# RWKV-7 and S5 decoder step on one core: S5 products and projection weight splits on VectorE, squares summed by TensorE, one function table for Ln and Exp

## The chip, the cores and the metric

The kernel runs on one of the eight cores of a Trainium2 chip. A core has a matrix engine (TensorE, PE in the rows), a vector engine (VectorE, DVE), an engine for activation functions (ScalarE, ACT), a general engine (GpSimd, POOL) and a queue that issues the transfers (SyncE, SP). Each runs its own list of instructions in order, and semaphores make one wait for another. The metric is the device time of one execution in microseconds (us), as the median of the runs.

## The reference, cut to what matters

One layer for a prompt of 1024 tokens and eight single-token samples, in float32. The two groups are joined to 1032 columns.

```python
h = rmsnorm(x, ln1_g); proj = h @ w_in       # 1024 -> 1792 (RWKV) + 512 (S5 input u) + 2048 (gates)
# RWKV-7: token shift, decay, normalised keys kk / |kk|, a matrix state per head, group norm of y
# S5: bu = B u per group, then s[t] = A s[t-1] + bu[t] in complex numbers, y = Re(C s) + D u
z = gelu(y_s5); zz = z @ w_glu; s5_out = zz[:, :D] * sigmoid(zz[:, D:])
x = x + (sigmoid(g_rw) * (y_rw @ w_rw_out) + sigmoid(g_s5) * s5_out) @ w_out
x = x + conv_ffn(rmsnorm(x, ln2_g))          # 1024 -> 2 x 2816, causal conv of width 3, gelu gate, down
x = x + sigmoid(rmsnorm(x, ln3_g) @ w_ple_gate) * (p @ w_ple)
y = rmsnorm(x, final_g)                      # rmsnorm: x * rsqrt(mean(x * x) + eps) * g
```

## The kernel before

Channels lie on the 128 partitions, tokens on the columns. A large product is exact to float32 in three faster passes: each operand is split into a rounded part "hi" and the rest "lo", and PE adds hi*hi, hi*lo and lo*hi in PSUM (mmblk). For the weights, ScalarE makes whi as a rounded copy and GpSimd makes wlo = raw - whi, 128x512 at a time (wload, line 490). A tile of the input projection takes 128 output channels: eight pieces of depth, three blocks of 344 columns, so 24 matmuls of 344 columns to a block. Its result in PSUM ("psm") is multiplied by rstd and carried to SBUF by VectorE: as "ut" for the four S5 input tiles, "pt" for the 14 RWKV tiles, "gt" for the 16 gate tiles. Eight low-rank products (xp, wp) are carried out by ScalarE ("st").

At the start, the eight pieces of x (128x1032, "xin") are scaled and split into h1h and h1l; ScalarE squares x in place (line 593); GpSimd adds the squares of pieces 1 to 3 and VectorE those of 5 to 7 into two sums, VectorE adds the two, and three fp32 products with a matrix of 1/1024 put the mean on all partitions ("pst", rstd1_ from line 600). rsqrt is Ln and then Exp, times -0.5 (line 527). Until rstd is there no projection block leaves PSUM: tile 0 has one block each in the pools pch, py and pb, and tile 1 has the three of pm.

The S5 part (build_s5) makes tables of powers of A (pr, pi, Q), the products wt, wx (for B) and cd, wy (for C), then the inputs of the state (be), and then runs the recurrence by cmac, which multiplies complex numbers in four products and four sums: first over 4 places at a time (three steps of 128x512), then over longer distances on VectorE alone, then back (four groups of 128x372). In the long steps two of the four products, ts[2] and ts[3], are on GpSimd. The first product of the outputs is "yp".

After that comes the RWKV stage, eight units of one head pair and half the tokens, each with several reciprocal roots and exponentials; the gate tiles and then the GLU fill PE between its small products. Behind it, two halves of 512 and 520 tokens run through the output products and the ConvFFN.

The order on each engine is not written by hand. Every operation is recorded by Sched.rec (all operations have line 413) with a priority, and Sched.run picks for the engine that is free first the ready operation with the lowest priority number, by estimated costs; S5 and RWKV (SIDE) go ahead of the projection tiles (MAIN), and results carried out of PSUM (HI) ahead of both. In Sched.issue a function that isn't in the present table set makes ScalarE switch: SETS lists the sets that hold a function, and the first of the list is taken.

```python
SETS = {"Exp": (0, 6), "Tanh": (0, 11), "Ln": (5, 6), "Gelu_apprx_tanh": (11,), "Sin": (9,)}
if o.aset and self.aset not in o.aset:
    self.aset = o.aset[0]
```

Of the kernel before, what the change touches and what calls it, by code (L numbers as in the profile page):

```python
# [17 lines left out]
P = 128  # L18
# [83 lines left out]
class Sched:  # L102
# [273 lines left out]
    def issue(self, t, o):  # L376
        e = o.eng
        self.pend[e].remove(o)
        cost = o.cost
        if o.aset and self.aset not in o.aset:  # L380
            self.aset = o.aset[0]
            t += 1283
        if o.mode and o.mode != self.mode:
            self.mode = o.mode
            t += self.SWITCH
        if o.port:
            t = max(t, self.held["POOL" if e == "DVE" else "DVE"] - 190)
            self.held[e] = t + o.lat
        for nm in o.alloc:
            q, _ = self.tile_slot[nm]  # L390
            q[0].remove(min(q[0]))
            q[1].remove(nm)
        self.free[e] = t + cost
        if e == "SP":
            st = max(self.dma_free, t + 900)
            self.dma_free = st + o.tail
            end = self.dma_free + 1300
        else:
            end = t + o.lat
        o.ready, o.nd = end, -1  # L400
        for u in o.users:
            u.ready = max(u.ready, end + self.lat(o, u))
            u.nd -= 1
            if u.nd == 0:
                self.pend[u.eng].append(u)
        for nm in o.tiles:
            self.left[nm] -= 1
            if self.left[nm] == 0:
                q, _ = self.tile_slot[nm]
                q[0].append(end + 250)  # L410
        for p in o.pools:
            self.pool_left[p] -= 1
        o.fn(*o.args, **o.kw)  # L413
        o.users = o.args = o.kw = None
# [11 lines left out]
def build(tc, I, O, dbg=None):  # L426
# [50 lines left out]
    def wload(src, n=W4):  # L477
        wp, nr, nw, alt = wts["pool"]
        wts["n"] = wts.get("n", 0) + 1
        with g.prio(HI):  # L480
            if alt and wts["n"] % 2:
                raw = wp.tile([P, TW], F32, name="wraw", tag="ta", bufs=2)
                G.memset(raw[:, 0:1], 0.0)
            else:
                raw = wp.tile([P, W4], F32, name="wraw", tag="wraw", bufs=nr)
            dma(raw[:, :n], src)
            hi = wp.tile([P, W4], F32R, name="whi", tag="whi", bufs=nw)
            S.activation(hi[:, :n], raw[:, :n], AF.Copy)
            lo = wp.tile([P, W4], F32R, name="wlo", tag="wlo", bufs=nw)
            G.tensor_tensor(lo[:, :n], raw[:, :n], hi[:, :n].bitcast(F32), op=SUB)  # L490
        return [(hi[:, j * P:(j + 1) * P], lo[:, j * P:(j + 1) * P]) for j in range(n // P)]

    def wtiles(src, nk):
# [39 lines left out]
    hs = ExitStack()  # L533
    hp = pool(hs, "hp", side="right")
    wts["pool"] = hp, 2, 3, True

    def slot(name, dt=F32R, shape=(NT,), tag="h"):
        t = hp.tile([P] + list(shape), dt, name=name, tag=tag, bufs=16 if tag == "h" else 1)
# [34 lines left out]

    XT = ("ur", "cdl", "yf", "xs", "zt", "cd", "wx", "ut")
    with g.prio(HI):
        acc, wpre = [], [wtiles(I["w_in"][M_U[0]], 8)]
        for k in range(8):
            if k == 4:
                wpre.append(wtiles(I["w_in"][M_U[1]], 8))
            x = sp.tile([P, NT], F32, name="xin", tag=XT[k], bufs=1)  # L580
            if XT[k] in ("xs", "zt", "cd"):
                V.memset(x[:, 0:1], 0.0)
            elif XT[k] in ("wx", "ut", "yf", "cdl"):
                G.memset(x[:, 0:1], 0.0)
            dma(x, I["x"][k])
            hi, lo = slot("h1h"), slot("h1l")
            if k % 2 == 0:
                V.tensor_scalar(hi, x, pc("ln1", k), None, op0=MUL)
            else:
                S.activation(hi, x, AF.Copy, scale=pc("ln1", k))  # L590
            V.scalar_tensor_tensor(lo, x, pc("ln1", k), hi.bitcast(F32), op0=MUL, op1=SUB)
            with g.prio(HI + 1):
                S.activation(x, x, AF.Square)
                if k in (0, 4):
                    acc.append(x)
                else:
                    (G if k < 4 else V).tensor_tensor(acc[-1], acc[-1], x, op=ADD)
            hx.append((hi, lo))

    def rstd1_():  # L600
        with g.prio(HI):
            for b in range(3):
                ps = pb.tile([P, BL], F32, name="pst", tag="big")
                sl = slice(b * BL, (b + 1) * BL)
                V.tensor_tensor(acc[0][:, sl], acc[0][:, sl], acc[1][:, sl], op=ADD)
                T.matmul(ps, ones, acc[0][:, sl], start=True, stop=True)
                rsqrt(rstd1[:, b * BL:(b + 1) * BL], ps, epst[:, 0:1])


    def win(m, evac, pools=None):  # L610
# [26 lines left out]
    def u_tile(q):  # L637
# [5 lines left out]
        def ev(b, sl, ps):  # L643
# [5 lines left out]
            if b == 2:  # L649
                V.tensor_tensor(ut[:, 0, 136:144], ps[:, 336:344], rstd1[:, NP:], op=MUL)  # L650
                V.tensor_tensor(ut[:, 7, 0:8], ps[:, 336:344], rstd1[:, NP:], op=MUL)
        win(M_U[q], ev, ((pch, "ch"), (py, "Y"), (pb, "big")) if q == 0 else None)
        with g.prio(HI):
            dma(dap(Ud[q], 0, [[144, P], [16 * 1152, 8], [1, 144]]), ut)

# [56 lines left out]
    for p in (2, 3):  # L712
        proj_tile(M_K[p])
        proj_tile(M_R[p])
        proj_tile(M_V[p])
    for m in M_GS + M_GR:
        gate_tile(m)

# [253 lines left out]
def build_s5(g, sp, pb, cp, I, O, Ud, Zd, pcs, dscr, dap, dma):  # L972
# [112 lines left out]
    frb = t["fr"][:, :, None].to_broadcast([P, 32, 16])  # L1085
    fib = t["fi"][:, :, None].to_broadcast([P, 32, 16])
    tt(v1, frb, Br, MUL)
    G.tensor_tensor(v2, fib, Bi, op=MUL)
    tt(b1, v1, v2, SUB)
    tt(v1, frb, Bi, MUL)  # L1090
    tt(v2, fib, Br, MUL)
# [13 lines left out]
    for q in range(4):  # L1105
# [3 lines left out]
        wx = tl("wx", [8, 9, 16], tag="wx")  # L1109
        V.tensor_tensor(wt, prr[:, gs, :, None].to_broadcast(sh),  # L1110
                        b1[:, gs, None, :].to_broadcast(sh), op=MUL)
        G.tensor_tensor(wx[:, :, 0:8], pir[:, gs, :, None].to_broadcast(sh),
                        b2[:, gs, None, :].to_broadcast(sh), op=MUL)
        V.tensor_tensor(wt, wt, wx[:, :, 0:8], op=ADD)
        bt = tl("bt", [8, 128], tag="bt")
# [9 lines left out]
        for i0 in (0, 3, 6):  # L1125
# [5 lines left out]
            for h in range(2):  # L1131
# [3 lines left out]
                for dst, r in zip(Xe, (0, 64)):  # L1135
# [3 lines left out]
                    else:  # L1139
# [4 lines left out]
        V.tensor_tensor(cd, q1[:, gs, :, None].to_broadcast(sh),  # L1144
                        Cr[:, gs, None, :].to_broadcast(sh), op=MUL)
        wx = tl("wy", [8, 9, 16], tag="ys")
        G.tensor_tensor(wx, q2[:, gs, :, None].to_broadcast(sh),
                        Ci[:, gs, None, :].to_broadcast(sh), op=MUL)
        V.tensor_tensor(cd, cd, wx, op=ADD)
        cdd = dscr(f"cdd{q}", [P, 8, 9, 16])  # L1150
# [20 lines left out]
        "p (a b c) -> p a b c", b=n[1], c=n[2]) if len(n) == 3 else \  # L1171
        m[i][:, :math.prod(n)].rearrange("p (a b) -> p a b", b=n[1])

    def cmac(outr, outi, ar, ai, br, bi, ts, small=False):
        E = V if small else G
        E.tensor_tensor(ts[2], ar, bi, op=MUL)
        V.tensor_tensor(ts[0], ar, br, op=MUL)
        E.tensor_tensor(ts[3], ai, br, op=MUL)
        V.tensor_tensor(ts[1], ai, bi, op=MUL)
        V.tensor_tensor(outr, outr, ts[0], op=ADD)  # L1180
        V.tensor_tensor(outi, outi, ts[2], op=ADD)
# [7 lines left out]
    for v in range(1, 4):  # L1189
        cmac(xv[0][:, :, :, v, 3], xv[1][:, :, :, v, 3], *qb(3, 8),  # L1190
             xv[0][:, :, :, v - 1, 3], xv[1][:, :, :, v - 1, 3],
             [mv(j, 16, 8) for j in range(4)], True)
    for u in range(1, 8):
        cmac(xv[0][:, :, u, 3, 3], xv[1][:, :, u, 3, 3], Qr[:, :, 15], Qi[:, :, 15],
             xv[0][:, :, u - 1, 3, 3], xv[1][:, :, u - 1, 3, 3],
             [m[j][:, :16] for j in range(4)], True)
    for v in range(3):
        cmac(xv[0][:, :, 1:, v, 3], xv[1][:, :, 1:, v, 3], *qb(4 * v + 3, 7),
             xv[0][:, :, :7, 3, 3], xv[1][:, :, :7, 3, 3],
             [mv(j, 16, 7) for j in range(4)], True)  # L1200

    x0 = tl("x0", [2, 16, 8])
    dma(x0, I["s5x0"])
# [1 line left out]
    dma(x0s, I["s5x0s"])  # L1205
    mv8 = [mv(j, 16, 8) for j in range(4)]
    ab8 = lambda z: z[:, :, None].to_broadcast([P, 16, 8])
    cmac(er, ei, ab8(apr), ab8(api), x0[:, 0], x0[:, 1], mv8, True)

    for i, e in enumerate((er, ei)):  # L1210
        S.activation(x0[:, i], e, AF.Copy)
# [520 lines left out]
```

## Time and profile before

| what | value |
| --- | --- |
| runs | 1912.15, 1913.16 and 1919.73 us, median 1913.16 |
| profiled execution | 1906.36 us |
| its span, from the first to the last instruction | 1904.6 us |
| mean granted TensorE clock | 0.973 of full speed |
| PE, DVE, ACT, POOL busy | 1829.4, 1159.5, 832.3, 847.0 us |
| function-table loads on ACT | 68, 87.2 us in all |

Busy is the time in which an engine has an instruction under way. Matmuls overlap each other, so a busy PE need not be at its full pace, and the count of matmuls in a stretch says more. An fp32 product shows as two matmul records.

### The profile page before, as it was taken

The numbers are of one execution on the slowest core, as the hardware profiler recorded it, in microseconds if no ns is written. First come the engines' busy times: TensorE is split into PE (matmuls) and PEld (weight loads), VectorE is DVE, ScalarE is ACT, GpSimd is POOL, SyncE is SP. The second block draws the span as 40 slices with busy tenths as digits, with TensorE's granted clock in tenths as the row PEclk, the third lists the DMA queues.
The fourth block names the chain that finished last, engine by engine and source line by source line (L and its number), as shares of the span: only waits on it lengthen the run. The fifth ranks groups of instructions, "written<-read, shape, count | busy, mean of one in ns | idle before, by whom it ended". The sixth has DMA issues, their size and how long they took to land.

```text
span 1904.6 us, 32427 instructions
## 1 busy us (share of the span) xinstructions
PE 1829.4 (96%) x11904; PEld 1624.1 (85%) x11904; DVE 1159.5 (61%) x2333; ACT 832.3 (44%) x1461; POOL 847.0 (44%) x1151
## 2 busy tenths in 40 slices
PE   6998899999999999999999999999999999999987
PEld 5987899877878889887788888888899999999987
DVE  8998527678666578777655534447555445444565
ACT  5232435346355465645633333335545333323354
POOL 4453325223223243336655454546564444444454
PEclk9998999899799999999999999999999999999988
DMA  5453684322123255344633333323332233233322
GB/s 189 145 169 113 186 256 130 112 78 81 53 78 95 74 176 158 90 156 137 211 101 113 114 97 97 94 94 112 100 123 78 90 92 98 90 95 96 90 70 87
DMA packets 157950, 219.81 MB, mean 115 GB/s; under 512 B 48208, under 2 KB 81488, under 8 KB 157648
## 3 DMA queue, kind: packets, MB, share of 16 engines
q1 hardware_dynamic: 157792, 217.74, 36.7%
q8 instruction: 94, 1.54, 0.3%
q14 instruction: 64, 0.52, 0.1%
HBM read 174.94 MB, written 42.92 MB: 114 GB/s over the span
## 4 chain that ended last, share of the span: by engine, by line
PE 77%; DVE 9%; DMA 6%; ACT 3%; issue 2%; POOL 1%; SPq 1%; DVEq 0%; POOLq 0%; ACTq 0%
PE psm L413 65%; PE chp L413 4%; PE Yps L413 2%; DVE Tm L413 1%; PE gp L413 1%; DVE Tt L413 1%; PE yp L413 1%; DVE x L413 1%; SPq L413 1%; DMA yf<-yq 1%; POOL wlo L413 1%; PE mgp L413 1%; ACT L413 1%; DVE m L413 1%; DVE Xi L413 1%
## 5 line engine op out<-in xcount | busy, mean ns | idle before, releaser
L413 POOL TENSOR_TENSOR wlo<-wraw,whi 128x512 fp32r<-128x512 f32 (+2 forms) x468 | 599.4, 1284 | 557.3 <-ACT whi L413 531.2
L413 PE MATMUL psm<-act,whi 128*128 128x260 f32 (+1 forms) x2880 | 655.2, 322 | 3.3 <-ACT whi L413 2.3
L413 PEld LDWEIGHTS psm<-act,whi 128*128 128x128 f32 x2880 | 480.2, 190 | 47.8 <-ACT whi L413 2.9
L413 ACT ACTIVATE whi<-wraw 128x512 fp32r<-128x512 f32 (+2 forms) x468 | 279.0, 598 | 526.5 <-PE psm L413 314.5
L413 PE MATMUL psm<-act,wlo 128*128 128x260 f32 (+1 forms) x1440 | 463.1, 322 | 0.5 <-POOL wlo L413 0.5
L413 PE MATMUL psm<-mid,whi 128*128 128x260 f32 (+1 forms) x1344 | 307.0, 321 | 2.0 <-ACT mid L413 2.0
L413 PEld LDWEIGHTS psm<-act,wlo 128*128 128x128 f32 x1440 | 273.4, 190 | 22.0 <-POOL wlo L413 0.9
L413 PE MATMUL psm<-h1h,whi 128*128 128x344 f32 x816 | 272.1, 336 | 12.9 <-DVE s_sh L413 9.7
L413 PE MATMUL psm<-h1h,wlo 128*128 128x344 f32 x816 | 274.0, 336 | 0.8 <-POOL wlo L413 0.8
L413 PE MATMUL psm<-h1l,whi 128*128 128x344 f32 x816 | 272.1, 334 | 2.0 <-DVE h1l L413 2.0
L413 PEld LDWEIGHTS psm<-mid,whi 128*128 128x128 f32 x1344 | 223.4, 189 | 23.5 <-ACT mid L413 2.6
L413 PE MATMUL psm<-mid,wlo 128*128 128x260 f32 (+1 forms) x672 | 214.6, 322 | 0.5 <-POOL wlo L413 0.5
L413 PEld LDWEIGHTS psm<-h1h,whi 128*128 128x128 f32 x816 | 159.0, 195 | 18.1 <-ACT s_sh L413 9.6
L413 PEld LDWEIGHTS psm<-h1l,whi 128*128 128x128 f32 x816 | 159.2, 195 | 4.9 <-DVE h1l L413 2.5
L413 PEld LDWEIGHTS psm<-h1h,wlo 128*128 128x128 f32 x816 | 159.1, 195 | 4.6 <-POOL wlo L413 1.1
L413 DVE TENSOR_TENSOR x<-psm,x 128x260 f32<-128x260 f32 (+1 forms) x160 | 84.6, 532 | 121.6 <-PE psm L413 121.5
L413 PEld LDWEIGHTS psm<-mid,wlo 128*128 128x128 f32 x672 | 126.5, 188 | 10.8 <-POOL wlo L413 0.9
L413 DVE TENSOR_TENSOR ta<-psm,rs 128x260 f32<-128x260 f32 (+1 forms) x66 | 34.0, 517 | 143.0 <-PE psm L413 131.1
L413 DVE SCALAR_TENSOR_TENSOR cv<-ta,par,cv 128x512 f32<-128x512 f32 x88 | 88.8, 1009 | 40.5 <-ACT cv L413 39.0
L413 ACT ACT_TABLE_LOAD x68 | 87.2, 1283 | 1.9 <-PEq L1723 0.7
L413 DVE TENSOR_TENSOR mid<-cv,mid 128x260 fp32r<-128x260 f32 (+1 forms) x84 | 69.5, 832 | 29.1 <-ACT mid L413 28.8
L413 ACT ACTIVATE sw<-S,WC 64x64 f32<-64x64 f32 x120 | 41.3, 344 | 73.1 <-DVE S L413 71.4
(346 smaller groups left out, 2578.0 us busy)
## 6 DMA issues: line engine op xcount, KB each, us to landing
wraw<-in_w_ffn_in SPq DMA_DIRECT2D x176, 256.0 KB, 2.6
wraw<-in_w_in SPq DMA_DIRECT2D x68, 256.0 KB, 3.5
wraw<-in_w_ffn_out SPq DMA_DIRECT2D x64, 192.0 KB, 2.4
gd<-gt SPq DMA_DIRECT2D x16, 516.0 KB, 3.1
wraw<-in_w_out SPq DMA_DIRECT2D x32, 256.0 KB, 2.7
wraw<-in_w_ple_gate SPq DMA_DIRECT2D x32, 256.0 KB, 2.7
wraw<-in_w_ffn_out SPq DMA_DIRECT2D x32, 256.0 KB, 3.0
pd<-pt SPq DMA_DIRECT2D x12, 516.0 KB, 3.4
```

Source lines behind the costliest of these rows:

```text
L413: o.fn(*o.args, **o.kw)
```

## The change

Four things change. In wload the low part of the weights is made by the engine in wts["lo"]: VectorE for the 18 tiles of S5 input and RWKV, GpSimd from the gate tiles on. In build_s5 all products are on VectorE: v2, wx, wy, and ts[2] and ts[3] of every cmac. The squares of x are summed by 24 fp32 products into three PSUM blocks that are taken from pb before the loop; tile 0 of the projection has a block of pm in place of the one of pb. And where a function is in set 6, which holds Ln and Exp, that set is loaded.

```diff
@@ issue
         if o.aset and self.aset not in o.aset:
-            self.aset = o.aset[0]
+            self.aset = 6 if 6 in o.aset else o.aset[0]
+            if self.aset == 6 and len(o.aset) > 1:
+                self.nc.scalar.preload_act_table_set("natural_log_exp_and_others")
             t += 1283
@@ wload
-            G.tensor_tensor(lo[:, :n], raw[:, :n], hi[:, :n].bitcast(F32), op=SUB)
+            wts["lo"].tensor_tensor(lo[:, :n], raw[:, :n], hi[:, :n].bitcast(F32), op=SUB)
@@ build
     wts["pool"] = hp, 2, 3, True
+    wts["lo"] = V
...
-        acc, wpre = [], [wtiles(I["w_in"][M_U[0]], 8)]
+        wpre = [wtiles(I["w_in"][M_U[0]], 8)]
+        pst = [pb.tile([P, BL], F32, name="pst", tag="big") for _ in range(3)]
         for k in range(8):
...
                 S.activation(x, x, AF.Square)
-                if k in (0, 4):
-                    acc.append(x)
-                else:
-                    (G if k < 4 else V).tensor_tensor(acc[-1], acc[-1], x, op=ADD)
+            for b in range(3):
+                T.matmul(pst[b], ones, x[:, b * BL:(b + 1) * BL], start=k == 0, stop=k == 7)
...
             for b in range(3):
-                ps = pb.tile([P, BL], F32, name="pst", tag="big")
-                sl = slice(b * BL, (b + 1) * BL)
-                V.tensor_tensor(acc[0][:, sl], acc[0][:, sl], acc[1][:, sl], op=ADD)
-                T.matmul(ps, ones, acc[0][:, sl], start=True, stop=True)
-                rsqrt(rstd1[:, b * BL:(b + 1) * BL], ps, epst[:, 0:1])
+                rsqrt(rstd1[:, b * BL:(b + 1) * BL], pst[b], epst[:, 0:1])
...
-        win(M_U[q], ev, ((pch, "ch"), (py, "Y"), (pb, "big")) if q == 0 else None)
+        win(M_U[q], ev, ((pch, "ch"), (py, "Y"), (pm, "psm")) if q == 0 else None)
...
+    wts["lo"] = G
     for m in M_GS + M_GR:
         gate_tile(m)
@@ build_s5
-    G.tensor_tensor(v2, fib, Bi, op=MUL)
+    tt(v2, fib, Bi, MUL)
...
-        G.tensor_tensor(wx[:, :, 0:8], pir[:, gs, :, None].to_broadcast(sh),
+        V.tensor_tensor(wx[:, :, 0:8], pir[:, gs, :, None].to_broadcast(sh),
...
-        G.tensor_tensor(wx, q2[:, gs, :, None].to_broadcast(sh),
+        V.tensor_tensor(wx, q2[:, gs, :, None].to_broadcast(sh),
...
-    def cmac(outr, outi, ar, ai, br, bi, ts, small=False):
-        E = V if small else G
-        E.tensor_tensor(ts[2], ar, bi, op=MUL)
+    def cmac(outr, outi, ar, ai, br, bi, ts):
+        V.tensor_tensor(ts[2], ar, bi, op=MUL)
         V.tensor_tensor(ts[0], ar, br, op=MUL)
-        E.tensor_tensor(ts[3], ai, br, op=MUL)
+        V.tensor_tensor(ts[3], ai, br, op=MUL)
```

Since the order follows from costs and readiness, it changes along with the work. On ScalarE, where rstd of the first norm is made (xin are the squares, rstd Ln and Exp of the sums), this stands there before:

```order
L413 ACTIVATE whi<-wraw 128x512 x2
L413 ACT_TABLE_LOAD
L413 ACTIVATE rstd_71<-pst,epst 128x344 x2
L413 ACT_TABLE_LOAD
L413 ACTIVATE rstd_71<-rstd_71 128x344 x2
L413 ACT_TABLE_LOAD
L413 ACTIVATE rstd_71<-pst,epst 128x344
L413 ACT_TABLE_LOAD
L413 ACTIVATE rstd_71<-rstd_71 128x344
```

and this in the change:

```order
L415 ACTIVATE xin<-xin 128x1032 x4
L383 ACT_TABLE_LOAD
L415 ACTIVATE rstd_71<-pst,epst 128x344 x2
L415 ACTIVATE rstd_71<-rstd_71 128x344 x2
L415 ACTIVATE rstd_71<-pst,epst 128x344
L415 ACTIVATE rstd_71<-rstd_71 128x344
```

Four loads became one, and the split of the weights (whi) moved from ahead of rstd to behind it.

On PE the sums of squares (pst) stand between the projection products of the first tiles (psm), before behind 144 of these:

```order
L413 MATMUL psm<-h1l,whi 128x344
L413 MATMUL psm<-h1h,wlo 128x344
L413 MATMUL pst<-xin,ones 128x344 x3
L413 MATMUL psm<-h1h,whi 128x344
L413 MATMUL psm<-h1l,whi 128x344
L413 MATMUL psm<-h1h,wlo 128x344
```

and in the change behind 35 of them:

```order
L415 MATMUL psm<-h1h,wlo 128x344
L415 MATMUL psm<-h1l,whi 128x344
L415 MATMUL pst<-xin,ones 128x344 x24
L415 MATMUL psm<-h1h,whi 128x344
L415 MATMUL psm<-h1l,whi 128x344
L415 MATMUL psm<-h1h,wlo 128x344
```

All 24 stand in one piece, and the products that wait for no rstd, 85 of them, are behind it.

On VectorE, in the first steps of the S5 recurrence (m are the products, Xr and Xi the states, pt a projection block carried out of PSUM), this stands there before, from one pt to the second next:

```order
L413 TENSOR_TENSOR pt<-psm,rstd_71 128x344
L413 TENSOR_TENSOR m_656<-Qr,Xr 128x512
L413 TENSOR_TENSOR m_657<-Qi,Xi 128x512
L413 TENSOR_TENSOR Xr<-Xr,m_656 128x16x32
L413 TENSOR_TENSOR pt<-psm,rstd_71 128x344
L413 TENSOR_TENSOR Xi<-Xi,m_658 128x16x32
L413 TENSOR_TENSOR Xr<-Xr,m_657 128x16x32
L413 TENSOR_TENSOR Xi<-Xi,m_659 128x16x32
L413 TENSOR_TENSOR m_656<-Qr,Xr 128x512
L413 TENSOR_TENSOR pt<-psm,rstd_71 128x344
```

and in the change from one pt on, the next one standing two rows behind the last shown:

```order
L415 TENSOR_TENSOR pt<-psm,rstd_71 128x344
L415 TENSOR_TENSOR m_659<-Qi,Xr 128x512
L415 TENSOR_TENSOR wlo<-wraw,whi 128x512
L415 TENSOR_TENSOR m_657<-Qi,Xi 128x512
L415 TENSOR_SCALAR st<-st 128x1032
L415 TENSOR_TENSOR Xr<-Xr,m_656 128x16x32
L415 TENSOR_TENSOR Xi<-Xi,m_658 128x16x32
L415 TENSOR_TENSOR Xr<-Xr,m_657 128x16x32
L415 MEMSET pt 128x1
L415 TENSOR_TENSOR Xi<-Xi,m_659 128x16x32
L415 TENSOR_TENSOR m_658<-Qr,Xi 128x512
L415 TENSOR_TENSOR m_656<-Qr,Xr 128x512
```

Two products more in each step, two of the weight splits (one shown, wlo) and a scaling (st) stand between the same evacuations.

On the other queues, SP issues the weight loads of the third tile ahead of the S5 constants (before: behind two of them), and up to the RWKV stage GpSimd has no instruction left but short fills of tiles.

## Rows read from the trace of the kernel before

**Rows 1.** Busy us of each engine, share of the span and instructions (the page)
```profile
PE 1829.4 (96%) x11904; PEld 1624.1 (85%) x11904; DVE 1159.5 (61%) x2333; ACT 832.3 (44%) x1461; POOL 847.0 (44%) x1151
```

**Rows 2.** By stage: stretch, length, busy PE, PEld, DVE, ACT, POOL, clock, DMA share
```profile
0.00:207.00 207.00, 180.48 (x1034) 164.81 (x1034) 185.02 (x383) 72.16 (x116) 96.27 (x105) 0.93 0.47 152
140.00:180.00 40.00, 33.12 (x139) 27.18 (x138) 34.59 (x90) 9.06 (x16) 16.46 (x13) 0.79 0.33 111
310.00:950.00 640.00, 627.11 (x4275) 524.25 (x4275) 446.97 (x1104) 330.21 (x581) 240.45 (x398) 0.97 0.38 115
950.00:1904.00 954.00, 928.75 (x6004) 845.11 (x6003) 486.38 (x771) 381.61 (x693) 478.50 (x582) 0.99 0.31 97
```

**Rows 3.** An undisturbed stretch, the projection products alone
```profile
60.00:80.00 20.00, 20.00 (x129) 1.00 0.47 142
```

**Rows 4.** Waits of PE up to 310 us: total us, times, longest
```profile
PE psm L413 <- DVE s_sh L413: 9.7, 1, 9.7
PE psm L413 <- DVE pt L413: 6.9, 2, 4.5
```

**Rows 5.** Timeline of VectorE: start us, us, engine, line, operation
```profile
11.54 2.49 DVE L413 SCALAR_TENSOR_TENSOR h1l<-xin,par,h1h 128x1032 fp32r<-128x1032 f32 x2
...
14.81 5.50 DVE L413 SCALAR_TENSOR_TENSOR h1l<-xin,par,h1h 128x1032 fp32r<-128x1032 f32 x2
...
113.73 1.35 DVE L413 TENSOR_TENSOR cd<-q,bc 128x1152 f32<-128x1152 f32 x1
...
142.85 0.49 DVE L413 TENSOR_TENSOR pt<-psm,rstd 128x344 f32<-128x344 f32 x1
...
148.05 1.07 DVE L413 TENSOR_TENSOR Xi<-Xi,m 128x512 f32<-128x512 f32 x1
...
149.99 0.52 DVE L413 TENSOR_TENSOR pt<-psm,rstd 128x344 f32<-128x344 f32 x1
```

**Rows 6.** Timeline of GpSimd beside the second pair of h1l
```profile
16.26 2.95 POOL L413 TENSOR_TENSOR xin<-xin 128x1032 f32<-128x1032 f32 x1 [0.41 <-ACT xin L413]
```

**Rows 7.** PE in four stretches: busy (records), granted clock, DMA share, GB/s
```profile
36.60:46.50 9.90, 3.82 (x9) 0.69 0.16 53
46.50:50.00 3.50, 3.42 (x12) 0.50 0.00 0
360.00:375.00 15.00, 13.61 (x72) 0.66 0.30 82
474.00:498.00 24.00, 24.00 (x109) 0.51 0.15 39
```

**Rows 8.** Chain of waits, S5 stage: start us, us, what, records
```profile
100.75 2.05 PE be L413 x16
```

**Rows 9.** Groups of VectorE up to 207 us: count, busy us, mean ns
```profile
L413 DVE SCALAR_TENSOR_TENSOR h1l<-xin,par,h1h 128x1032 fp32r<-128x1032 f32 x8 | 18.2, 2308 | 0.3
...
L413 DVE TENSOR_TENSOR cd<-cd,wy 128x1152 f32<-128x1152 f32 x4 | 9.1, 2287 | 0.2
...
L413 DVE TENSOR_TENSOR cd<-q,bc 128x1152 f32<-128x1152 f32 x4 | 8.2, 2060 | 0.0
...
L413 DVE TENSOR_TENSOR wt<-wt,wx 128x1024 f32<-128x1024 f32 x4 | 4.8, 1211 | 0.0
...
L413 DVE TENSOR_TENSOR wp<-wraw,wp 128x512 fp32r<-128x512 f32 x2 | 1.3, 674 | 0.0
```

**Rows 10.** Function-table loads (the page): count, busy us, mean ns, idle before
```profile
L413 ACT ACT_TABLE_LOAD x68 | 87.2, 1283 | 1.9 <-PEq L1723 0.7
```

**Rows 11.** Timeline of ScalarE in the RWKV stage
```profile
357.37 1.28 ACT L413 ACT_TABLE_LOAD   x1
358.67 0.63 ACT L413 ACTIVATE sq<-sq 128x512 f32<-128x512 f32 x1
359.20 0.57 ACT L413 ACTIVATE Gm<-mgp 32x512 f32<-32x512 f32 x1
```

**Rows 12.** Waits of PE in the RWKV stage
```profile
PE chp L413 <- ACT Gm L413: 1.5, 2, 1.0
```

More of the change, by code (lines that the diff above doesn't have):

```diff
@@ L1191, in build_s5 @@
              xv[0][:, :, :, v - 1, 3], xv[1][:, :, :, v - 1, 3],
-             [mv(j, 16, 8) for j in range(4)], True)
+             [mv(j, 16, 8) for j in range(4)])
     for u in range(1, 8):
@@ L1195, in build_s5 @@
              xv[0][:, :, u - 1, 3, 3], xv[1][:, :, u - 1, 3, 3],
-             [m[j][:, :16] for j in range(4)], True)
+             [m[j][:, :16] for j in range(4)])
     for v in range(3):
@@ L1199, in build_s5 @@
              xv[0][:, :, :7, 3, 3], xv[1][:, :, :7, 3, 3],
-             [mv(j, 16, 7) for j in range(4)], True)
+             [mv(j, 16, 7) for j in range(4)])
     x0 = tl("x0", [2, 16, 8])
@@ L1207, in build_s5 @@
     ab8 = lambda z: z[:, :, None].to_broadcast([P, 16, 8])
-    cmac(er, ei, ab8(apr), ab8(api), x0[:, 0], x0[:, 1], mv8, True)
+    cmac(er, ei, ab8(apr), ab8(api), x0[:, 0], x0[:, 1], mv8)
     for i, e in enumerate((er, ei)):
```

## The prediction

> **What bounds the kernel now.** I read the busy shares first [rows 1]: TensorE (PE) is busy 1829.4 of 1904.6 us, VectorE (DVE) 61%, GpSimd (POOL) and ScalarE (ACT) 44% each. So the end is set by PE's own work plus the time in which PE waits or runs slowly, and work of another engine counts only where PE waits for it. Next I read busy time by stage [rows 2]: from 950 us on PE has 929 of 954 us, from 310 to 950 it has 627 of 640; but from 140 to 180 us it has 33.1 of 40 at a mean granted clock of 0.79. In the first 207 us (up to the first product of the S5 outputs, "yp") DVE is busy 185 us. The pace of an undisturbed stretch is 129 matmuls in 20 us, 0.155 us each [rows 3].
>
> The waits of PE say who holds it up [rows 4]: 9.7 us before the first matmul, 6.9 us for "pt", a projection block that DVE carries out of PSUM. So PE waits because DVE comes late. Why DVE is late is seen in its timeline [rows 5]: two h1l of 1032 columns took 2.49 us (1.25 each), the next two 5.50, while GpSimd among other things added up squares [rows 6]. Between the evacuations at 142.85 and 149.99 us DVE worked 7.1 us on adds and products of the S5 recurrence; one alone takes 1.07. Instructions of DVE and POOL that both read two SBUF tiles stretch each other.
>
> A wait costs PE more than its length [rows 7]: after the idle stretch 36.6 to 46.5 us the granted clock is 0.50 (1.2 instead of 2.4 GHz) from 46.5 to 50, and 12 matmuls run where the pace gives 22.
>
> **The change part by part.** The sum goes against the profiled execution, 1906.36 us (span 1904.6 and 1.8 around it); the median of the runs, 1913.16, is 1.0036 times that.
>
> (a) Squares summed by PE. In place of 3 fp32 products there are 24 of 344 columns. Eight fp32 products of the S5 part, 136 columns each, take 2.05 us in 16 records [rows 8], 0.256 each, so 344 columns take 0.65 at full clock: 24 x 0.65 = 15.6 us, less about 3.4 now (3.82 busy, less three ordinary ones at 0.155) [rows 7]: +12. They cover no idle time: in the new order they stand in one block behind 35 projection products, where PE has other work ready. Bounds: +5 if most of it replaces waits for h1l, +28 at half clock.
>
> (b) The first product waits longer. DVE now does two weight splits before it (0.67 each, the duration of "wp", same shape [rows 9]) and the short S5 instructions that stood behind it, between 9.7 us [rows 4] and 11.5 us [rows 5]: +3. The bounds are 0 and +3.3. From there all h1l run without GpSimd beside them, so the last Square should end near 26 us (the first product at 12.7, then by DVE's rows 8 x 1.25 for h1l, three h1h at about 0.75 and one split).
>
> (c) The wait for rstd goes. From 36.6 to 46.5 us PE is busy 3.8 of 9.9, and the half clock behind it costs 1.6 (10 matmuls): -7.7. What is late next is the evacuation of the first blocks, at about 35 us (squares products from 18 to 33, then Ln, Exp); but PE then has 85 projection products (13 us) left for the five blocks that have PSUM, so it should not stop. Bounds -7.7 and -3.
>
> (d) The S5 stage, 140 to 180 us. 139 records at 0.155 are 21.5 us of the 40; I count 16 as lost, since the low-rank products among them are slower by themselves. DVE takes over 21 splits before the first yp (x 0.67 = 14), v2 and eight wx and wy (0.67 + 4 x 1.21 [rows 9] + 4 x 1.35 [rows 5] = 11), six 128x512 products (x 1.07 = 6) and eight of 372 columns (half of that each, an estimate: 4): +35. It loses the six sums of squares (3 x 1.25 + 3 x 0.42, from h1l by columns: 5) and the stretching. By group means [rows 9] that is 8 x (2.31 - 1.25) = 8.5 for h1l and 4 x (2.29 - 1.35) + 4 x (2.06 - 1.35) = 6.6 for the two cd groups: 15 from three groups; all of GpSimd's 96 busy us [rows 2] are the other end. I take 30, near the lower end, as the other groups are smaller: DVE's load stays as it is. What matters then is the spacing of evacuations. Where four instructions stand between two of them now (7.1 us), twelve stand then, by rows some 11 us (nine at 1.07, a split, a scaling at about 0.7). PE has three buffers of 24 products, 11 us of work, so it still waits, but less long: I take half of the 16, -8. Bounds -16 and +6.
>
> (e) The other waits for evacuations between 46 and 207 us, some 7 us in all: -3. Bounds -7 and +4.
>
> (f) One table for Ln and Exp. The program's order has 69 function-table loads before and 42 after, 27 x 1.28 us = 35 us less on ACT [rows 10]; not more, since each Tanh or Gelu between brings the other table back. ACT is no bound. What counts is a place like that at 357 us [rows 11]: a load and a reciprocal root stand ahead of "Gm", for which PE waits [rows 12], and from 360 to 375 us the clock is 0.66, that is 5 us lost; 474 to 498 us at 0.51, 12 us lost [rows 7], has no load just ahead of it. In the new order no load stands between the first two units: -6. Bounds +6 (another such stretch appears) and -20 (both go). The Trainium skill, page "ScalarE: Activation LUTs", section "What ACT_TABLE_LOAD costs", puts a switch at 2.66 us with its drain; here the load is 1.28 and the next instruction starts 0.02 us behind it [rows 11], so the trace does not show that drain. By the page this term would be about -9.
>
> Sum: +12 + 3 - 7.7 - 8 - 3 - 6 = -9.7. I forecast -11, as the lower bounds of (d) to (f) lie farther off than the upper ones: 1895.4, times 1.0036 is 1902 us.
>
> **Rivals.** 1, a larger gain: DVE is freed by far more than 30 us, so the waits of (d) go whole, and with them both half-clock stretches of (f): 12 + 3 - 7.7 - 16 - 5 - 17 = -31, 1882 us. For it: PE's waits named here are for DVE, and DVE is stretched by more than twice in rows 5. Against: the new spacing of evacuations.
>
> 2, a trade: what GpSimd gives up DVE has to do, one instruction after the other as before; the waits of (d) and (e) stay, and (f) gives 3: 12 + 3 - 7.7 - 3 = +4, 1917 us, no change. For it: 185 of 207 us of DVE are busy already. The Trainium skill, page "Perfetto Trace Analysis", section "Optimizing Scalar/DVE Operations", warns that moving work between these two engines might not help, since they share a read port; the rows agree on the sharing, but 1.25 against 2.75 us for one h1l says that ending the overlap gives something back.
>
> 3, slower: DVE becomes the bound of the S5 stage. It decides from the point where DVE's time to the first yp exceeds PE's. PE's is 12.7 + 742 x 0.155 + 160 short S5 records x 0.128 [rows 8] + 15.6 = 164 us; if only the 15 us of stretching counted above go, DVE's is 185 + 35 - 5 - 15 = 200 and some 8 before it has anything to do. The first yp, which with 126 products fewer ahead of it (19.5 us) would come at 187.5 at today's speed, then comes at 208: +20 with (f) at 0, 1933 us. For it: ten instructions of 1 us between two evacuations. Against: GpSimd's 96 us would then have cost DVE only 15, which rows 5 make unlikely.
>
> **How the numbers follow.** Forecast 0.5 (its own range -19 to -3 us), rival 1 0.13, rival 2 0.25, rival 3 0.12. Less than 0.5% (9.5 us) can't be told from no change: 0.37 of the forecast's half lies beyond it, which with rival 1 makes 0.50 faster; 0.13 and rival 2 make 0.38 the same; 0.12 slower. The range, 1881 to 1920, holds the forecast, rival 2 and half of rival 1.
>
> **What would show it.** (a) 24 squares products in one block, 15 to 17 us long, at clock 1.0. (b) The first matmul near 12.7 us. (c) The first "ut" near 35 us, and PE without a long gap from 13 to 50. (d) h1l at 1.25 us throughout, PE's wait for pt below 4 us, and the first yp near 183 us (187.5 less (a) to (e)). (f) 27 table loads fewer, and no clock of 0.66 near 360 us. The forecast is wrong if PE still waits 7 us or more for pt (then rival 2 or 3), or if the squares run at 1.2 GHz.

## The result, and the profile after

The changed kernel took 1924.35 us (median of 20 runs, 1911.49 to 1938.47) against 1911.9 us for the kernel before (20 runs, 1896.76 to 1921.64): ratio 1.0086, with a 95% interval of 1.0064 to 1.0108. It is slower by about 16 us (the means of the runs are 1925.5 and 1909.7); 1902 us had been forecast, with a range up to 1920. The profiled execution took 1918.17 us (span 1916.4), 11.8 more than that of the kernel before.

The page of the changed kernel, busy time by engine, to be set beside [rows 1]:

```profile
PE 1852.4 (97%) x11946; PEld 1637.8 (85%) x11946; DVE 1135.4 (59%) x2386; ACT 799.5 (42%) x1434; POOL 734.4 (38%) x1089
```

POOL lost 113 us of work and ACT 33 us, DVE gained none, and PE is busy 23 us longer. So PE's idle time fell from 75.2 to 64.0 us (span less busy), and the loss is in time in which PE is busy. Before any stage is blamed, the signs of the prediction are looked up one by one. First the waits of PE up to 310 us, to be read against [rows 4]:

```profile
PE psm L415 <- DVE h1h L415: 11.3, 1, 11.3
PE ssp L415 <- ACT kkn L415: 6.6, 1, 6.6
...
PE psm L415 <- DVE pt L415: 2.4, 3, 1.5
```

The wait for pt is down from 6.9 to 2.4 us, as forecast (below 4). The first product stands at 11.3 us (12.7 forecast, 9.7 before). Next come the squares on PE, the first block carried out by VectorE, and two h1l together (timeline of the changed kernel; three answers, of PE, DVE and DVE):

```profile
19.87 14.04 PE L415 MATMUL pst<-xin,ones 128*128 128x344 f32 x48
```
```profile
35.90 0.77 DVE L415 TENSOR_TENSOR ut<-psm,rstd 128x344 f32<-128x344 f32 x1
```
```profile
14.55 2.50 DVE L415 SCALAR_TENSOR_TENSOR h1l<-xin,par,h1h 128x1032 fp32r<-128x1032 f32 x2
```

The 24 products stand in one block. The next product starts at 33.49 us, so they take 13.6 us. The first ut comes at 35.9 us (35 forecast), and h1l takes 1.25 us everywhere, where [rows 5] had 2.75 beside GpSimd. Now the stages of the changed kernel (columns as in [rows 2]):

```profile
0.00:186.70 186.70, 169.30 (x950) 150.83 (x950) 168.67 (x421) 65.88 (x108) 4.82 (x55) 0.96 0.47 156
140.00:180.00 40.00, 39.09 (x188) 34.19 (x189) 39.07 (x153) 12.57 (x24) 0.53 (x6) 0.87 0.43 142
279.80:848.50 568.70, 557.60 (x3914) 466.56 (x3913) 389.91 (x1050) 260.66 (x482) 177.47 (x309) 0.95 0.31 94
848.50:1916.40 1067.90, 1043.50 (x6571) 941.32 (x6569) 536.81 (x844) 429.44 (x778) 538.40 (x671) 0.99 0.34 108
```

The first yp stands at 186.7 us (207.5 before, 183 forecast), and from 140 to 180 us PE has 39.09 of 40 us instead of 33.12. So most signs of the front came as the prediction says, and the loss comes later. The RWKV stage runs here from 279.8 us (first chp) to 848.5 us (last of its records). In the kernel before, the same stage and what follows are these two rows:

```profile
308.20:925.30 617.10, 606.76 (x4201) 508.63 (x4200) 435.31 (x1090) 314.49 (x554) 225.49 (x374) 0.97 0.36 108
925.30:1904.60 979.30, 950.90 (x6092) 862.22 (x6090) 499.85 (x789) 399.02 (x723) 493.45 (x605) 0.99 0.33 102
```

The stage is shorter now by 48 us, and that misleads: it also holds 305 projection products fewer (1764 instead of 2069), which come later instead. To compare stages, I take from the length of each the time that its projection products need at their undisturbed pace (0.1555 us for 344 columns, 0.118 for 260, 0.230 for 512). What remains is the price of everything else:

| remainder in us | before | changed | difference |
| --- | --- | --- | --- |
| start to first yp | 72.5 | 71.4 | -1.1 |
| to first chp | 38.5 | 38.3 | -0.2 |
| RWKV stage | 275.5 | 294.4 | +18.9 |
| rest | 56.2 | 50.4 | -5.8 |
| sum | 442.7 | 454.5 | +11.8 |

The difference of the sums is that of the two executions. In the RWKV stage the records of the granted clock show 34.1 us at half clock before and 61.4 us now; over the whole span they show 103.0 and 113.9, since the other stages have less of it now. The longest of these stretches in the changed kernel, all engines and then the projections alone (busy PE, PEld, DVE, ACT, clock, DMA):

```profile
549.80:580.50 30.70, 30.70 (x118) 22.48 (x118) 11.82 (x37) 8.62 (x19) 3.63 (x9) 0.50 0.14 38
```
```profile
549.80:580.50 30.70, 12.76 (x33) 9.23 (x33) 0.52 (x1) 0.00 (x0) 0.50 0.14 38
```

PE is busy all the time, but with 33 projections among 118 records. What came just before, in the timeline of the same kernel:

```profile
546.29 1.17 PE L415 MATMUL mgp<-av,Gm 32*32 32x32 f32 x32 [0.82 <-DVE av L415]
547.38 0.48 PE L415 MATMUL gp<-AR,BK 64*128 64x128 f32 x2
...
548.62 1.19 PE L415 MATMUL mgp<-Gm,av 32*32 32x32 f32 x32
549.74 0.78 PE L415 MATMUL gp<-AR,BK 64*128 64x128 f32 x2
550.45 2.07 PE L415 MATMUL gps<-sg,g 128*128 128x512 f32 x2
```

Small products of RWKV follow each other (32x32 in groups of 32) with four projections among them, where the dots stand, and the clock falls behind them. The function-table loads did go as forecast, from 69 (68 of them in the group of [rows 10]) to 42 (groups of ScalarE in the changed kernel):

```profile
L415 ACT ACT_TABLE_LOAD x22 | 28.2, 1283 | 1.2 <-PEq L1721 0.7
L383 ACT ACT_TABLE_LOAD x19 | 24.4, 1283 | 0.3
L332 ACT ACT_TABLE_LOAD x1 | 1.3, 1283 | 0.0
```

### The profile page after: what moved, and what is told of

The parts are those of the page before. It is cut to its first block, busy times and chain, and to the rows that moved or that the text cites. A ratio compares the mean times of both kernels' runs of the same rounds, so it can differ in the third digit from the quotient of the medians.

```text
span 1916.4 us, 32539 instructions
## 1 busy us (share of the span) xinstructions
PE 1852.4 (97%) x11946; PEld 1637.8 (85%) x11946; DVE 1135.4 (59%) x2386; ACT 799.5 (42%) x1434; POOL 734.4 (38%) x1089
## 4 chain that ended last, share of the span: by engine, by line
PE 73%; DVE 10%; DMA 4%; ACT 3%; issue 2%; POOL 1%; SPq 1%; DVEq 0%; ACTq 0%; POOLq 0%
PE psm L415 61%; PE chp L415 5%; PE Yps L415 2%; PE gp L415 1%; DVE m L415 1%; DVE act L415 1%; SPq L415 1%; DMA wraw<-in_w_rw_out 1%; PE yp L415 1%; DVE x L415 1%; DVE Tm L415 1%; DVE Tt L415 1%; POOL wlo L415 1%; DVE Xi L415 1%; DVE Xr L415 1%
## 5 line engine op out<-in xcount | busy, mean ns | idle before, releaser
L415 POOL TENSOR_TENSOR wlo<-wraw,whi 128x512 fp32r<-128x512 f32 (+2 forms) x432 | 541.0, 1255 | 499.6 <-ACT whi L415 430.4
L415 PE MATMUL psm<-mid,whi 128*128 128x260 f32 (+1 forms) x1344 | 303.0, 320 | 0.0
L415 PE MATMUL psm<-h1h,whi 128*128 128x344 f32 x816 | 273.5, 337 | 12.4 <-DVE h1h L415 11.3
L415 PE MATMUL psm<-zh,whi 128*128 128x344 f32 x192 | 63.1, 328 | 4.3 <-DVE gt L415 4.0
```

## The experiments

Two theories stood at the start. Theory 1: the planner's new order of the RWKV stage costs the time, by the clock. Theory 2: the front of the kernel (squares on PE, splits on DVE) costs it. Ratios are to the kernel before, timed on the same chip, with 95% intervals; "clock" is the mean granted clock of the runs compared (the kernel before: 0.971 to 0.974; the changed kernel: 0.967).

**The function table.** e1 is the kernel before with the table rule alone:

```diff
-            self.aset = o.aset[0]
+            self.aset = 6 if 6 in o.aset else o.aset[0]
+            if self.aset == 6 and len(o.aset) > 1:
+                self.nc.scalar.preload_act_table_set("natural_log_exp_and_others")
             t += 1283
```

> The kernel before with the new function-table rule alone (POOL keeps its splits and products, squares are summed as before). Theory 1, the planned order: the rule takes 1.28 us off the planner's clock at many Ln and Exp, so it puts the eight RWKV units closer together; between the first and the last chp stand 1719 projection products (psm) instead of 1890, the small RWKV products run back to back in more places, and TensorE's clock is halved there for longer. Then this part alone is slower: about +8 us on the kernel before (ratio 1.003 to 1.007), with 50 us or more at half clock between 280 and 880 us. Theory 2, the front of the kernel: the squares on PE and the splits on DVE cost more than they free, and the table rule gains what was predicted, -6 us (ratio 0.997).

e2 loads by the new rule (self.real) but plans by the old one, so that no engine's order changes:

```diff
+        if o.aset and self.real not in o.aset:
+            self.real = 6 if 6 in o.aset else o.aset[0]
+            if self.real == 6 and len(o.aset) > 1:
+                self.nc.scalar.preload_act_table_set("natural_log_exp_and_others")
         if o.aset and self.aset not in o.aset:
             self.aset = o.aset[0]
             t += 1283
```

> The kernel before, every engine's order unchanged (the planner counts by the old rule), but the shared table is loaded wherever it will do: 46 table loads in the order instead of 69. Theory 1: the loads that go are worth little, 0 to -5 us, and half clock between 300 and 880 us stays about as before (34 us). Theory 2: the gain is that of the loads, the same -6 us as with the rule alone.

e1: 1.0048 (1.0018 to 1.0078), clock 0.967, with 68 us at half clock in the RWKV stage. e2: 1.0008 (0.9978 to 1.0037), clock 0.974. So the loads that go are worth nothing that can be measured, and the rule costs 9 us by the order alone. The trace of e2 also shows the place that the prediction had in mind. In the kernel before, a load stands just ahead of the reciprocal root and Gm [rows 11]; in e2 it is gone (ScalarE, then PE with busy time, records, clock, DMA share and GB/s):

```profile
356.03 0.62 ACT L417 ACTIVATE sq<-sq 128x512 f32<-128x512 f32 x1
356.79 0.59 ACT L417 ACTIVATE Gm<-mgp 32x512 f32<-32x512 f32 x1
```
```profile
359.40:376.50 17.10, 16.84 (x68) 0.50 0.34 99
```

The half clock is there all the same, 17.1 us long where the records before show 10.2, so the load ahead of Gm was not its cause.

**The rest of the change.** e3 is the changed kernel without the table rule (the hunk of e1 reversed), e4 has in its place the loads of e2.

> The changed kernel without the new table rule (squares on PE, S5 products and splits on DVE stay). 1764 projection products stand between the first and the last chp (1560 in the changed kernel, 1890 before). Theory 1: as fast as the kernel before or up to 5 us faster, some 12 us faster than the changed kernel, with about 35 us at half clock in the RWKV stage. Theory 2: slower still than the changed kernel, about +16 us on the kernel before (ratio 1.008 to 1.012).

> The changed kernel with the table loads of the new rule (48 in the order) but planned by the old one, so that its order is that of the kernel without the table rule. Theory 1: about 0 to -8 us on the kernel before, the best of the four. Theory 2: 6 us less than the kernel without the rule, still +10 us on the kernel before.

e3: 1.0048 (1.0020 to 1.0076). Theory 1 had it as fast as the kernel before, theory 2 slower than the changed one; it is neither. e4: 1.0067 (1.0034 to 1.0099), against theory 1 as I had put it. By these ratios the table rule makes up less than half of the loss (1.0086 less 1.0048).

e5 takes the squares alone, e6 S5 products and splits alone, e7 those with GpSimd's three sums of squares on VectorE too (the main lines of each edit):

```diff
 e5: +            for b in range(3):
     +                T.matmul(pst[b], ones, x[:, b * BL:(b + 1) * BL], start=k == 0, stop=k == 7)
 e6: +    wts["lo"] = V
     -        E = V if small else G
     +        E = V
 e7: -                    (G if k < 4 else V).tensor_tensor(acc[-1], acc[-1], x, op=ADD)
     +                    V.tensor_tensor(acc[-1], acc[-1], x, op=ADD)
```

> The kernel before with the squares summed by TensorE alone (POOL keeps its splits and products, old table rule). Theory 1: the 24 products cost PE 13.6 us (24 x 0.567 in the changed kernel) in place of 3.8 and what they free does not pay for it: +5 to +10 us on the kernel before when both are taken at one mean granted clock, so the squares are the part that costs without the table rule. Theory 2, the load on DVE: the squares take sums off DVE and POOL and end the wait for rstd, so they are worth -4 to 0 us, and it is the splits and S5 products on DVE that cost +9.

> The kernel before with S5 products and weight splits on VectorE alone (squares summed as before, old table rule). Theory 1: no more work for PE and less waiting in the first 207 us: 0 to -6 us on the kernel before at one mean granted clock (ratio 0.997 to 1.000). Theory 2: +9 us (ratio 1.005), with PE's waits for pt above 7 us.

> As the kernel with S5 products and splits on VectorE, and the three sums of squares of GpSimd on VectorE as well (no squares on PE, GpSimd nearly idle in the first 200 us, old table rule). Theory 1: the h1l of the first 30 us take 1.25 us each, the sums end earlier, and it is as fast as its neighbour or up to 4 us faster. Theory 2: three more adds of 1032 columns on DVE (about 1.1 us each) make it 3 us slower than its neighbour.

e5: 1.0065 (1.0030 to 1.0100), clock 0.971. e6: 0.9926 (0.9897 to 0.9955), clock 0.981. e7: 0.9924 (0.9892 to 0.9956), clock 0.982, 1896.56 us; it beats both kernels. Its front and its RWKV stage:

```profile
0.00:191.00 191.00, 171.32 (x982) 157.71 (x983) 178.56 (x435) 69.28 (x112) 5.56 (x56) 0.95 0.50 163
285.90:877.40 591.50, 578.94 (x4149) 489.75 (x4148) 416.85 (x1081) 301.89 (x533) 199.63 (x351) 0.99 0.35 108
```

The front's remainder is 64.1 us (72.5 before); the stage's clock is 0.99 with 10 us at half clock. e11 and e12 split e6 into its two halves (the main line of each):

```diff
 e11: -        E = V if small else G
      +        E = V
 e12: +    wts["lo"] = V
```

> The kernel before with the S5 products alone on VectorE (splits on POOL, squares and table rule as before). Its order from the RWKV stage on is, on PE, DVE and ScalarE, the same as that of the kernel with the squares alone on PE. Theory 1: so its mean granted clock is that kernel's 0.971 within 0.002, and its time is less by the squares' 10 us: about 1911 us, ratio 1.000 to 1.003. Theory 2: the gain of S5 products and splits (ratio 0.993) comes mostly from this part, ratio about 0.995.

> The kernel before with the weight splits of the input projections alone on VectorE (S5 products on POOL, squares and table rule as before). 604 projection products stand before the first yp (868 before), 1785 among the RWKV products. Theory 1: its order in the RWKV stage is about as thin as that of the kernel before, so mean granted clock 0.972 to 0.975 and 1905 to 1912 us, ratio 0.998 to 1.002. Theory 2: the splits carry half of the gain, ratio about 0.996.

e11: 1.0006 (0.9981 to 1.0032), clock 0.974. e12: 1.0018 (0.9989 to 1.0046), clock 0.970. Each half alone is worth nothing, both together 14 us. On PE, e11 has the order of e5 from the first chp on, record by record, and nearly its clock (0.974 and 0.971); the two ratios differ by 0.6%, of which part is that difference in clock. The same holds for the kernel before and e2 (0.974 both) and for e3 and e4 (0.973 and 0.972): with one order of the RWKV stage the mean clocks lie within 0.003 of each other, and over all orders tried they go from 0.954 to 0.982. e9 is the changed kernel with its squares summed as before (the lines of e5 reversed):

> The changed kernel with the squares summed as before (POOL and DVE adds, one fp32 product for each block); S5 products, splits and the new table rule stay. Theory 1, two separate prices (squares: 10 us of PE work; planned order of the RWKV stage: what half clock it leaves): 1670 projection products stand among the RWKV products and more places are thin than without the table rule, so mean granted clock about 0.972 and 1908 to 1913 us, ratio 1.000 to 1.002. Theory 2, the parts simply add: 0.9926 for S5 products and splits times 1.0048 for the rule, 0.997, 1902 us.

1.0028 (1.0005 to 1.0051), clock 0.970: the parts don't simply add.

**The order alone.** e8 and e10 let the planner put a projection between small products (e8: after six in the changed kernel, shown here; e10: after four in e7):

```diff
+            if e == "PE":
+                main = [c for c in cand if c[0] <= t + 1e-6 and c[1].prio >= MAIN]
+                if self.thin >= 6 and main:
+                    r, o = min(main, key=lambda c: (c[1].prio, c[1].seq))
+                self.thin = 0 if o.cost > 140 else self.thin + 1
```

> The changed kernel with one more rule for the planner: after six small RWKV products in a row on PE it issues a projection product that is ready, whatever its priority. 1671 projection products stand between first and last chp, 1560 in the changed kernel. Theory 1 (thin stretches of the RWKV stage let the clock fall): less half clock between 280 and 850 us than the changed kernel's 61 us, mean granted clock up by 0.002 to 0.004, 3 to 6 us faster than the changed kernel (ratio to the kernel before about 1.006). Theory 2: the RWKV stage's order is not what costs, the ratio stays at 1.0086.

> The fast kernel with S5 products, splits and all sums on VectorE, with the planner's fill rule (after four small RWKV products it issues a projection product that is ready). The work is the same, only the order in the RWKV stage differs: 1820 projection products among the RWKV products instead of 1782, but they are spent early in a unit, so that later in it there are more places where small products stand nearly alone (none in the plan without the rule). Theory 1 (thin places set the clock): mean granted clock falls from 0.982 to about 0.971, some 15 us slower than without the rule, ratio about 1.000 to the kernel before. Theory 2 (what counts is how many projections stand among the RWKV products): the same or faster, ratio 0.992 or below.

e8: 1.0040 (1.0009 to 1.0071); its interval meets that of the changed kernel (from 1.0064), so the gain that theory 1 expected is not shown. e10: 1.0257 (1.0216 to 1.0298), clock 0.954: the sign of theory 1, but by the ratios some 64 us slower than e7 where 15 were expected. Its work is that of e7, and so is its front; only the order of the RWKV stage differs:

```profile
0.00:191.10 191.10, 170.55 (x982) 156.55 (x983) 178.76 (x435) 69.54 (x112) 5.26 (x56) 0.96 0.50 163
289.30:949.30 660.00, 649.09 (x4197) 535.28 (x4196) 425.67 (x1088) 306.52 (x539) 206.07 (x357) 0.92 0.33 99
```

The same 982 records in front take 191 us in both; the stage takes 660 us instead of 591.5, with 109 us at half clock instead of 10. Part of that is no matter of the clock. In the timeline of e10, where the granted clock is 1.00 until 443.9 us, a projection now stands between groups of eight mgp:

```profile
441.69 0.43 PE L419 MATMUL mgp<-av,Gm 32*32 32x32 f32 x8
442.06 0.42 PE L419 MATMUL psm<-h1h,whi 128*128 128x344 f32 x1
442.41 0.43 PE L419 MATMUL mgp<-av,Gm 32*32 32x32 f32 x8
```

while e7 has the 32 in one piece:

```profile
430.94 1.19 PE L413 MATMUL mgp<-av,Gm 32*32 32x32 f32 x32
432.06 0.50 PE L413 MATMUL vps<-yl,bor 128*128 128x512 f32 x1
```

In e10 eight mgp and a projection take 0.72 us from start to start, so 32 with four projections 2.9 us; in e7 that would be 1.12 + 4 x 0.1555 = 1.7 us. There are 16 such groups of 32, so up to 18 us go into changes between the two kinds.

Last, the work of the change with other orders. Only times that the planner assumes are altered: for a change of the products' tile shape (SWITCH), and until PE can use a result of another engine (LATE).

```diff
 e13: -    LATE = {"PE": 200, "DVE": 35, "ACT": 35, "POOL": 70, "SP": 60}
      +    LATE = {"PE": 400, "DVE": 35, "ACT": 35, "POOL": 70, "SP": 60}
      -    SWITCH = 90
      +    SWITCH = 45
 e14: -    SWITCH = 90
      +    SWITCH = 150
```

> The changed kernel, work untouched, two of the planner's assumed times altered: 45 instead of 90 ns for a change of the products' tile shape on PE, and 400 instead of 200 ns until a result of another engine can be used on PE. The order has 1948 projection products among the RWKV products (1560 in the changed kernel) and few places where small products stand nearly alone. Theory 1 (the order of the RWKV stage and the clock it leaves make most of the loss): half clock in that stage below 35 us (61 in the changed kernel), mean granted clock 0.976 or more, 1905 us or less, ratio 0.995 to 1.001, in spite of the squares on PE. Theory 2 (the parts of the change cost it, the order only scatters): ratio stays at 1.006 to 1.010.

> The changed kernel, work untouched, with the planner's assumed time for a change of tile shape on PE at 150 instead of 90 ns: 1445 projection products among the RWKV products and twice as many places where small products stand nearly alone. Theory 1: more half clock in the RWKV stage than the changed kernel's 61 us (80 or more), mean granted clock about 0.960, ratio 1.015 or more. Theory 2: ratio stays at 1.006 to 1.010.

> The changed kernel without the table rule, planned with 400 instead of 200 ns until a result of another engine can be used on PE: 1845 projection products among the RWKV products (1764 without that), almost no place where small products stand nearly alone. Theory 1: mean granted clock about 0.979, ratio 0.995 to 1.000 where the same work stood at 1.0048. Theory 2: ratio 1.003 to 1.007 as before.

e13: 0.9982 (0.9959 to 1.0005), clock 0.978: the whole change, 20 us faster than the changed kernel by order alone, and as fast as the kernel before. e14: 1.0190 (1.0146 to 1.0234), clock 0.957. Their RWKV stages, e13 first:

```profile
281.30:916.40 635.10, 624.51 (x4314) 529.01 (x4314) 433.32 (x1099) 291.59 (x535) 216.70 (x366) 0.97 0.34 106
```
```profile
281.60:850.00 568.40, 558.28 (x3810) 463.95 (x3810) 374.32 (x1043) 255.23 (x475) 174.69 (x303) 0.91 0.30 90
```

They hold 2165 and 1662 projections, and 44 and 102 us at half clock. e13's profiled execution shows more half clock than the 35 us expected, at a clock of 0.975 where its runs have 0.978. e15, the change without the table rule and with LATE at 400 for PE, stayed at 1.0053 (1.0027 to 1.0078), clock 0.972: a miss. Its order has hardly a place where small products stand nearly alone, and yet 48 us are at half clock. So that count, which I read off the order, does not foretell the clock.

What holds over the kernels is the link from half clock to time. The remainder of the RWKV stage and its half clock are in us, each from one profiled execution; the ratio is that of the runs. The last column is explained below the table:

| kernel | half clock | remainder | ratio | at one clock |
| --- | --- | --- | --- | --- |
| e7 | 10.2 | 272.7 | 0.9924 | +3.1 |
| e6 | 23.9 | 276.5 | 0.9926 | +2.2 |
| before | 34.1 | 275.5 | 1 | 0 |
| e13 | 44.4 | 283.5 | 0.9982 | +4.2 |
| e5 | 47.8 | 284.6 | 1.0065 | +12.0 |
| e3 | 58.0 | 288.5 | 1.0048 | +9.2 |
| changed | 61.4 | 294.4 | 1.0086 | +8 |
| e1 | 68.3 | 293.0 | 1.0048 | +0.2 |
| e9 | 71.7 | 297.8 | 1.0028 | +4.3 |
| e14 | 102.4 | 310.0 | 1.0190 | +10.7 |
| e10 | 109.2 | 330.0 | 1.0257 | +24.1 |

e8's profiled execution lies 12 us above the median of its runs and is left out. A line through the other sixteen profiles has the slope 0.51: about half of the time at half clock is lost, with some 5 us to either side and 12 for e10. The Trainium skill, page "TensorE: Matmul & The Clock Gate", section "Terms", puts the penalty at the throttled time times the share of pulses that is cut; the profiles agree.

The runs allow a second reading that does not hang on single executions. Within one kernel, a run whose mean granted clock is lower by 0.001 takes 1.55 us longer (fitted to 288 runs, each taken against the mean of its kernel; scatter 2 us). With this price the last column brings the runs of each kernel to one clock and gives what is left of the difference to the kernel before, an estimate with some 2 us to either side, more for e10 and e14. (The clock of the 20 runs of the kernel before that belong to the result is not known; for the changed kernel the other runs of the kernel before stand in.) So of the 16 us of the changed kernel about 8 are clock and 8 are not. e1 loses by the clock alone, e6 and e7 gain by the clock alone, while e5 and e3 are slower at nearly the clock of the kernel before. e11, not in the table, stands at +8.4 and made up for it by its clock; e12 stands at +1.3. e10's +24 against +3 for e7 fits the up to 18 us for changes between kinds of products.

## Why the prediction was wrong, point by point

Neither of the two signs of being wrong that the prediction named came: the wait for pt is 2.4 us, and the squares ran at full clock.

(a) The squares: right, somewhat too high. 13.6 us in place of 3.8 are +9.8; +12 was forecast.

(b) Right in sign, +1.65 instead of +3.

(c) The wait for rstd went: PE has no gap from 36.6 to 46.5 us any more, and the first ut is 1 us later than forecast.

(d), (e) The waits in the S5 stage went more fully than forecast (39.09 of 40 us busy). Together with (a) to (c) the front was to gain 3.7 us; up to the first chp it gained 1.3 in the profile. How much the squares take of that is bounded by three pairs: the remainder up to the first yp is higher with them by 5.4 us (e5 against before), 3.3 (e3 against e6) and 7.9 (changed against e9). Over the whole kernel and at one clock the same pairs give 12, 7 and 4 us. So (a) less (c), forecast as +4, lies at the lower end of what was measured.

(f) This step failed. It put the half clock near 360 us down to the load ahead of Gm [rows 11, 12], and took 6 us for the loads that go, with +6 as the upper bound. The loads were worth nothing, and the half clock stayed without the load (e2); the changed kernel has it too at the same place of its order, from 324.5 to 331.3 us, with no load ahead of its Gm. What the rule did was to shift the order: the planner counts each load at 1.28 us, so without them it sets the RWKV units closer, and of the projections between the first and the last chp (1890 before) 1719 are left in e1 and 1560 in the changed kernel. That cost 9 us (e1), all of it by the clock, where a bound of +6 stood. By the Trainium skill, page "ScalarE: Activation LUTs", section "What ACT_TABLE_LOAD costs", the term would have been -9; e2 does not bear that out either.

The larger fault lies beside the steps: I let the order of the RWKV stage change for (f) alone. The edits of the front and the table rule move it, and in the table the half clock of that stage goes from 10 to 72 us by them alone (e7, e9), some 32 us of time at a slope of 0.51, against 4 us forecast for the whole front. That is why e6 gains 14 us, in the main why the parts don't add, and why the same work comes out at 0.9982, 1.0086 or 1.0190 with mean clocks of 0.978, 0.967 and 0.957 (e13, changed, e14). It is not the whole loss: in the profiled executions PE is busy 23 us longer, of which the squares are 9.8 and the half clock over the whole span some 5.5 (10.9 us more, at 0.51); for the other 8 no run shows the cause. PE's shorter idle time gave back 11. No rival had this: the slower one put the loss into VectorE in the S5 stage, and the changed kernel's row from 140 to 180 us shows PE busier there than [rows 2]. The range ended at 1920 us, just above rival 2; (f) held one further half-clock stretch at most (+6).

In the front, moving work from GpSimd to VectorE paid: the h1l that had taken 2.75 us fell to 1.25, and the front's remainder by 4.9 us in e6, with 20.5 us at half clock there instead of 27.3. The Trainium skill's warning cited for the trade (page "Perfetto Trace Analysis", section "Optimizing Scalar/DVE Operations") is not borne out by this part; but at one clock the whole of e6 is 2 us slower, so the front's gain doesn't show in its time, and the 11 us of (d) and (e) are not confirmed by it.

What stays open: which feature of the order makes the clock fall, and what the 8 us of PE's busy time are that neither the squares nor the clock explain. Neither the number of projections in the stage (2047 in e10 with 109 us at half clock, 1764 in the changed kernel with 61) nor the count of thin places (e15) tells it beforehand. Of the 5.8 us that the rest of the kernel gave back, its half clock (27.9 us before, 21.7 now) is worth some 3; the others are open.

## What to carry to other kernels

Where a planner sets the order by assumed times, an edit in one place re-times all that follows; compare the order of the later stages, and above all the long stretches of small products on PE, before believing a sum made of the edited stage. Take apart a change of several parts by making each alone and by holding the order fixed (as e2 does): here one part gained 14 us, two lost 9 and 12, and the whole looked like a slow front. Where runs differ in their mean clock, compare kernels at one clock as well: the part that gained 14 us gained them by the clock, and the one that lost 12 lost them by its work. And once the work is settled, try a few values of the planner's assumed times: of three trials one was worth 20 us (e13), one nothing clear of noise (e15 against e3), and one cost 20 (e14).

## What the runs showed of the hardware

The clock was halved while PE was busy throughout (30.70 of 30.70 us from 549.8 us on), not only behind waits. One kernel's executions differ by it: the changed kernel's fastest run took 1911.49 us at a mean clock of 0.976, its slowest 1938.47 us at 0.956. And the first products run at half pace (timeline of the changed kernel):

```profile
13.08 0.49 PE L415 MATMUL psm<-h1h,wlo 128*128 128x344 f32 x1
13.37 0.49 PE L415 MATMUL psm<-h1h,whi 128*128 128x344 f32 x1
```

From start to start that is 0.29 us, against 0.155 a few us later. A window there shows a granted clock of 1.00, but the records of the clock begin only at 17.3 us in this trace, so that figure rests on no record; in the kernel before they begin at 16.42 us, and the products go from 0.29 to 0.16 us at 16.2 to 16.5.
